# Unread matmuls in TensorE's waits of a recurrent layer, an early output projection, and 512-column matmuls in block 1

## The chip, the cores and the metric

The kernel runs on one core of a Trainium2 chip. The metric is device microseconds for one execution. Engines: TensorE (PE in the profile; its weight loads are PEld), VectorE (DVE), ScalarE (ACT), GpSimd (POOL) and SyncE (SP), which issues the large loads.

## The reference, cut to what matters

256 tokens of width 1024, float32 throughout. Two blocks run one after the other.

```python
# block 1: two layers, each a mix of three branches
proj = rmsnorm(x, norm_g) @ w_in        # 256 x 1024 times 1024 x 8704
aq, ak, av, az, buv, bz, cq, ck, cv, cz, gl = split_cols(proj)
...                                      # two attentions, a gated unit
x = x + merged @ w_out
# block 2: 16 meta tokens + 256 tokens; two layers of ffn, mixer, ffn
h = h + 0.5 * swiglu_ffn(rms_norm(h, ..), ..)
h = h + mixer(rms_norm(h, ..))           # layer 0: attention + delta rule
h = h + 0.5 * swiglu_ffn(rms_norm(h, ..), ..)   # layer 1: rwkv7_time_mix
# rwkv7_time_mix, 16 heads of 64
xr, xw, xk, xv, xa, xg = [h + xx * mu[i] for i in range(6)]
r, k, v = xr @ w_r, xk @ w_k, xv @ w_v   # and three low-rank products
S = S * w_t + sa * b_t + v_t * k_t       # a recurrence over the tokens
y = S @ r_t                              # then a norm per head and a bonus
return (y * g) @ w_o
```

## The kernel before, in words

**Products.** A float32 product is made of three float32r matmuls that add in one PSUM bank: high part by high part, high by low, low by high (`mm3`, L216 to L220: L218, L219, L220). The weights come as units of 512 KB, 128 x 1024, in the order in which the kernel uses them (`Stream`, L192 to L213): SyncE issues the load into `wraw` (four buffers), ScalarE copies it to `wh` (L210, three buffers), VectorE or GpSimd subtracts to get `wl` (L212, three buffers).

**Block 1.** `block1_layer` runs for each of the two layers. In it `proj_tok` (L387 to L406) makes seven of the projections, q, k and v of the two attentions and one more: tokens are the stationary side (`xh`, `xl`, 128 tokens of one k-tile), and a half of the 512 output columns is the moving side. So one projection is two column halves `p`, two halves of k `kh`, two token halves `i`, four k-tiles, three matmuls of 256 columns each, into two banks. Each unit holds four k-tiles of 256 columns. The generator yields after each group of three, and a `Weave` runs other work of the layer between the yields. The order of the units in memory is written by the host (L1824 to L1832).

**Order and banks.** An instruction made through `Pinned` (L88 to L96) stays behind the instruction that was traced before it on its engine; all its records have line L96. All other instructions are put in order by a scheduler. PSUM is eight banks of 128 x 512 float32; `bank(c, tag)` takes the next bank of a ring that the tag names, each bank is a buffer tag of its own with one buffer, and its tiles are handed out in the order in which they were traced.

**The rwkv layer** (`rwkv`, L1479 to L1776, 272 tokens). Its head: statistics of the norm (`rms_scale`, TensorE lines L264), `replicate` of the scale to all partitions (L278 transposes through `rtok`), then the six mixes (L1512 to L1527, VectorE with halves on ScalarE and GpSimd), the three large projections and the low-rank ones. Then eight pairs of heads, j = 0 to 7, in five chunks of 64 tokens, run as a pipeline of three stages written out in a loop:

```python
for s in range(KT + 3):
    if 1 <= s <= KT:
        stage_b(s - 1, Cs[s - 1])
    if s >= 3:
        stage_c(s - 3, Cs[s - 3])
    if s < KT:
        Cs[s] = stage_a(s)
```

`stage_a` (L1650 to L1704) scales the operands on VectorE, makes the products of the pair (L1677: `bbd`, then `kbd`, each five of 128 x 128 in two tiles with tag `sm`), masks them on VectorE, reduces to `iUc` (L1690), transposes (L1696) and makes the bonus (L1702, `mk`). `sm` is a ring of two banks. `stage_b` inverts a triangle per chunk (`tri_inverse`, L910 to L953): 15 rounds of three small VectorE instructions (L923, L924, L925), a mask to `iY` (L927), then two levels of transposes (L937) and products (L946) on TensorE with VectorE's L949 and L951. `stage_c` (L1709 to L1763) runs the recurrence over the chunks (L1715 to L1737), then the norm of the heads (L1743, L1747) and the elementwise end that leaves `kk` and `kp`, the high and the low part of the pair's output (L1762 on ScalarE, L1763 on GpSimd). Buffers of stage A come round after four pairs; `iY` has two buffers.

**The output projection** (`out_proj`, L1779 to L1793) is called behind the loop (L1773) for 256 tokens with the tags `sm` and `iv`. It has eight units of 128 output rows; each adds eight head pairs, k = 0 to 7, three matmuls a pair, and VectorE adds the result to `h` (L1791).

Of the kernel before, what the change touches and what calls it, by code (L numbers as in the profile page):

```python
# [16 lines left out]
P = 128  # L17
D = 1024
KT = 8
# [60 lines left out]
def banks(c, **n):  # L80

    free = sorted(range(8), key=lambda i: c.used[i])
    c.banks = {}
    for tag, k in n.items():
        c.banks[tag], free = free[:k], free[k:]


class Pinned:  # L88
# [167 lines left out]
def rms_scale(c, acc, tok, r=None):  # L256

    nc = c.nc
    tt = tok_tiles(tok)
    nt = len(tt)  # L260
    ps = bank(c, "sm")
    for i, a in enumerate(tt):
        for q, t in enumerate(acc):
            nc.tensor.matmul(ps[:, i:i + 1], t[:, a:a + P], c.cmean, start=q == 0, stop=q == len(acc) - 1)  # L264
    ms = T(c, c.np_, [P, 4], F32, "ms")
    nc.vector.tensor_scalar_add(ms[:, :nt], ps[:, :nt], EPS)
    if r is None:
        r = T(c, c.np_, [P, 4], F32, "rtok")
    nc.gpsimd.tensor_tensor(r[:, :nt], ms[:, :nt], c.mhalf[:, :nt], ALU.pow)
    return r  # L270


def replicate(c, r, tok, R=None):

    nc = c.nc
    ps = bank(c, "sm")
    for i, a in enumerate(tok_tiles(tok)):
        nc.tensor.matmul(ps[:, a:a + P], r[:, i:i + 1].to_broadcast([P, P]), c.ident, start=True, stop=True)  # L278
    if R is None:
        R = T(c, c.np_, [P, tok], F32, "R", bufs=1)  # L280
    nc.scalar.activation(R, ps[:, :tok], AF.Copy)
    return R
# [89 lines left out]
def block1_layer(c, l, xT, head, pos, ws, w_br, w_out, sgu_w, sgu_b, sgu_gb):  # L372

    nc, tc, ap, tp = c.nc, c.tc, c.b1a, c.b1t
    lam_init = 0.8 - 0.6 * math.exp(-0.3 * l)
    xh, xl, acc = head
# [6 lines left out]
    def next_unit():  # L383
        unit[0] += 1
        return ws.unit(unit[0] - 1)

    def proj_tok(evac):  # L387

        pss = [bank(c), bank(c)]
        for p in range(2):  # L390
            for kh in range(2):
                wh, wl = next_unit()
                wh4 = wh.rearrange("p (m k c) -> p m k c", m=2, k=4)
                wl4 = wl.rearrange("p (m k c) -> p m k c", m=2, k=4)
                for i in range(2):
                    o = pss[i][:, 256 * p:256 * p + 256].rearrange("p (m c) -> p m c", m=2)
                    for k4 in range(4):
                        k = 4 * kh + k4
                        a, b = xh[:, k, P * i:P * i + P], xl[:, k, P * i:P * i + P]
                        h, w = wh4[:, :, k4, :], wl4[:, :, k4, :]  # L400
                        pe.matmul(o, a, h, start=k == 0, stop=False)
                        pe.matmul(o, a, w, start=False, stop=False)
                        pe.matmul(o, b, h, start=False, stop=k == 7)
                        if p and kh and k4 == 3:
                            evac(i, pss[i])
                        yield  # L406

    def rope_T(res, scale):

# [1069 lines left out]
def rwkv(c, h, acc, a):  # L1479
# [19 lines left out]

    with ExitStack() as fst:  # L1500
        fp = fst.enter_context(tc.tile_pool(name="rwf", bufs=1, reuse_waits="tile"))
        r = rms_scale(c, acc, TOK2)
        R = replicate(c, r, TOK2)
        lora1, lora2, wrkv = Stream(c, a["rw_lora1"]), Stream(c, a["rw_lora2"]), Stream(c, a["rw_rkv"])
        z1h, z1l = T(c, fp, [P, TOK2], F32R, "z1h"), T(c, fp, [P, TOK2], F32R, "z1l")
        zgh, zgl = T(c, fp, [P, 2, TOK2], F32R, "zgh"), T(c, fp, [P, 2, TOK2], F32R, "zgl")
# [113 lines left out]
    ys = []  # L1620
# [29 lines left out]
    def stage_a(j):  # L1650
        C = Ctx()
        D = Dall[:, j]
        E1 = T(c, pp, [P, NCH, 65], F32, "E1")
        nc.scalar.activation(E1, D, AF.Exp)
        E2 = T(c, pp, [P, NCH, 64], F32, "E2")
        nc.scalar.activation(E2, D[:, :, 1:], AF.Exp, scale=-1.0)
        C.fc = T(c, pp, [P, 4, 1], F32, "fc", bufs=4)
        nc.vector.tensor_sub(C.fc, D[:, 0:4, 64:65], D[:, 1:5, 0:1])
        nc.scalar.activation(C.fc, C.fc, AF.Exp)

        w = j % 4
        AR, Br, Kr, Ka = C.AR, C.Br, C.Kr, C.Ka = arp[w], brp[w], krp[w], kap[w]
        C.abd, C.bt, C.vt, C.kt = abdp[w], btp[w], vtp[w], [t[:, q] for c0, n, t in ktp[w] for q in range(n)]
        nc.vector.scalar_tensor_tensor(AR[:, :, 0, :], chv("kk", j), -1.0, E1[:, :, 0:64], ALU.mult, ALU.mult)
        halves(lambda o, x, p: nc.vector.tensor_mul(o, x, E2[p:p + 64]), bbd, chv("ba", j))
        nc.vector.tensor_mul(AR[:, :, 1, :], chv("r", j), E1[:, :, 1:65])
        halves(lambda o, x, p: nc.gpsimd.tensor_mul(o, x, E2[p:p + 64]), kbd, chv("kp", j))
        halves(lambda o, x, p: nc.scalar.activation(o, x, AF.Copy), C.abd, AR[:, :, 0, :])
        halves(lambda o, x, p: nc.gpsimd.tensor_copy(o, x), vbd, chv("v", j))

        Ub = C.Ub = ubp[j % 3]
        U16 = T(c, pp, [P, NCH, 64], F32, "fk")
        for bd, oa, orr in ((bbd, Ub, Br), (kbd, Ka, Kr)):
            for c0, m in ((0, 4), (4, 1)):
                ps = bank(c, "sm")
                for q in range(m):
                    nc.tensor.matmul(ps[:, P * q:P * q + P], pair_ht(bd[:, c0 + q]), pair_ht(AR[:, c0 + q]),  # L1677
                                     start=True, stop=True)
                p4 = ps[:, :P * m].rearrange("p (c a t) -> p c a t", a=2, t=64)
                if oa is Ub:  # L1680
                    nc.vector.tensor_mul(U16[:, c0:c0 + m, :], p4[:, :, 0, :],
                                         c.m16.unsqueeze(1).to_broadcast([P, m, 64]))
                if oa is Ka or c0 == 0:
                    nc.vector.tensor_mul(oa[:, c0:c0 + m].rearrange("p c (h t) -> p c h t", h=2),
                                         p4[:, :, 0:1, :].to_broadcast([P, m, 2, 64]),
                                         c.mU.rearrange("p (h t) -> p h t", h=2).unsqueeze(1).to_broadcast([P, m, 2, 64]))
                nc.vector.tensor_mul(orr[:, c0:c0 + m, :], p4[:, :, 1, :], c.mR.unsqueeze(1).to_broadcast([P, m, 64]))
            if oa is Ub:
                C.Uc = T(c, pp, [P, NCH, 16], F32, "iUc", bufs=3)
                nc.vector.tensor_reduce(C.Uc, U16.rearrange("p i (b c) -> p i c b", c=16), AX.X, ALU.add)  # L1690

        for bd, parts in ((bbd, [(0, 4, C.bt)]), (kbd, ktp[w]), (vbd, [(0, 4, C.vt), (4, 1, C.vt[:, 4:])])):
            for c0, m, tk in parts:
                ps = bank(c, "sm")
                for q in range(m):
                    nc.tensor.transpose(ps[:, P * q:P * q + P], pair_ht(bd[:, c0 + q]), c.ident)  # L1696
                nc.scalar.activation(tk[:, :m, :], ps[:, :P * m].rearrange("p (c d) -> p c d", d=P), AF.Copy)

        mk = T(c, pp, [P, NCH, 64], F32, "fk").rearrange("p c t -> p (c t)")[:, :TOK2]
        nc.vector.scalar_tensor_tensor(mk, tok("r", j), col(c, "r_k", j), tok("kp", j), ALU.mult, ALU.mult)  # L1700
        ps = bank(c, "sm")
        nc.tensor.matmul(ps[:, :TOK2], c.bo, mk, start=True, stop=True)  # L1702
        nc.vector.tensor_mul(tok("r", j), ps[:, :TOK2], tok("v", j))
        return C  # L1704
# [61 lines left out]
    for s in range(KT + 3):  # L1766
# [3 lines left out]
            stage_c(s - 3, Cs[s - 3])  # L1770
        if s < KT:
            Cs[s] = stage_a(s)
    acc2 = out_proj(c, h, ys, a["rw_out"], ("sm", "iv"), 16)  # L1773
    pst.close()
    st.close()
    return acc2  # L1776


def out_proj(c, h, ys, w_out, tags=("mm",), t0=0):  # L1779

    nc = c.nc
    wo = Stream(c, w_out)
    acc2 = []
    n = TOK2 - t0
    for m in range(KT):
        wh, wl = wo.unit(m)
        ps = bank(c, tags[m % len(tags)])
        for k in range(KT):
            mm3(c, ps[:, :n], wh[:, P * k:P * k + P], wl[:, P * k:P * k + P], *[y[:, t0:] for y in ys[k]],
                k == 0, k == KT - 1)  # L1790
        nc.vector.tensor_add(h[:, m, t0:], ps[:, :n], h[:, m, t0:])  # L1791
        sumsq(c, acc2, h[:, m, t0:], m, n)
    return acc2  # L1793
# [21 lines left out]
def b1_host(I):  # L1815
# [8 lines left out]
    order = []  # L1824
    for nm in ["cq", "ck", "cv", "aq", "ak", "av", "bz", "bu", "bv", "cz", "gC", "gB", "az", "gA"]:
        if nm[1] in "qkv":
            for p in range(2):
                for kh in range(2):
                    order += [(4 * kh + k4, base[nm] + 2 * p + m) for m in range(2) for k4 in range(4)]
        else:  # L1830
            for m in range(8 if nm[0] == "g" else 4):
                order += [(k, base[nm] + m) for k in range(8)]  # L1832
# [131 lines left out]
```

## Time and profile before

| what | us |
|---|---|
| three runs | 2038.01, 2035.98, 2027.44 (median 2035.98) |
| the profiled execution | 2033.22 |
| its span | 2031.5 |
| TensorE busy | 1929.5 (95%) |
| VectorE busy | 1390.8 (68%) |
| ScalarE busy | 973.2 (48%) |
| GpSimd busy | 285.1 (14%) |

Mean granted clock of TensorE in the profiled execution: 0.964 of its full speed. Times in the rows below are microseconds from the span's start. Matmuls are pipelined, so a matmul's own duration is longer than the distance from it to the next; a rate is read from starts. A row of the timeline is the start, the duration of the group, engine, line, operation, what is written from what, the tile and the count; in brackets how long the engine was idle before it and what ended that.

### The profile page before, as it was taken

What the parts mean: (1) busy time and instruction counts of PE and PEld (TensorE: products, weight loads), DVE (VectorE), ACT (ScalarE), POOL (GpSimd) and SP (SyncE); (2) the same over time, 40 slices, a digit from 0 to 9 for tenths busy, and PEclk for the clock granted to TensorE, in tenths of its full rate; (3) what the DMA queues carried; (4) which work ended last, traced back from release to release, by engine and by line L of the source; (5) the groups of instructions that cost most, each with busy time, mean ns of one, the idle gap of its engine ahead of it and who ended that gap; (6) DMA issues with size and microseconds to landing.
All of it is one profiled execution on the core that took longest, in us unless ns stands there. A gap on an engine that the chain in (4) does not pass through costs nothing.

```text
span 2031.5 us, 37801 instructions
## 1 busy us (share of the span) xinstructions
PE 1929.5 (95%) x15003; PEld 1858.0 (91%) x15003; DVE 1390.8 (68%) x2896; ACT 973.2 (48%) x1745; POOL 285.1 (14%) x320
## 2 busy tenths in 40 slices
PE   8999999999999999968999999999989879989998
PEld 7889999889999999966999999999988768979998
DVE  6577576577578665787477665666589699846764
ACT  5455355455355444442354444444366535555443
POOL 1113011113010000143010000000044313110000
PEclk9999899999899999987999999999989789989999
DMA  6445466445455555532235555555534100026663
GB/s 200 137 123 160 142 180 181 142 117 161 141 177 176 177 175 174 164 107 63 63 112 169 175 175 176 171 175 174 171 94 135 42 12 1 32 72 180 186 186 115
DMA packets 79461, 280.02 MB, mean 138 GB/s; under 512 B 9890, under 2 KB 12082, under 8 KB 79156
## 3 DMA queue, kind: packets, MB, share of 16 engines
q1 hardware_dynamic: 77088, 275.57, 45.5%
q8 instruction: 118, 1.93, 0.4%
q10 hardware_dynamic: 2196, 2.03, 0.3%
q14 instruction: 59, 0.48, 0.1%
HBM read 276.50 MB, written 1.07 MB: 137 GB/s over the span
## 4 chain that ended last, share of the span: by engine, by line
PE 64%; DVE 9%; ACT 2%; POOL 2%; issue 1%; DVEq 0%; ACTq 0%; POOLq 0%
PE mm L220 17%; PE mm L218 16%; PE mm L219 16%; PE mm L96 4%; PE iv L96 1%; PE iv L946 1%; DVE wl L212 1%; PE fs L96 1%; PE sm L1677 1%; DVE mixt L1523 1%; DVE iYc L925 1%; DVE ish L924 1%; DVE ish L923 0%; PE sm L264 0%; ACT wh L210 0%
## 5 line engine op out<-in xcount | busy, mean ns | idle before, releaser
L210 ACT ACTIVATE wh<-wraw 128x1024 fp32r<-128x1024 f32 x517 | 546.9, 1059 | 603.6 <-PE mm L219 288.8
L212 DVE TENSOR_TENSOR wl<-wraw,wh 128x1024 fp32r<-128x1024 f32 x474 | 587.1, 1239 | 254.9 <-ACT wh L210 249.6
L218 PE MATMUL mm<-xh,wh 128*128 128x272 f32 (+1 forms) x2112 | 607.4, 288 | 5.9 <-ACT xh L1524 3.0
L220 PE MATMUL mm<-xh,wl 128*128 128x272 f32 (+1 forms) x2112 | 606.2, 287 | 6.6 <-DVE wl L212 2.9
L219 PE MATMUL mm<-xl,wh 128*128 128x272 f32 (+1 forms) x2112 | 606.9, 287 | 0.9 <-POOL xl L1526 0.9
L220 PEld LDWEIGHTS mm<-xh,wl 128*128 128x128 f32 x2112 | 401.5, 190 | 9.0 <-DVE wl L212 5.1
L218 PEld LDWEIGHTS mm<-xh,wh 128*128 128x128 f32 x2112 | 399.7, 189 | 7.9 <-ACT xh L1524 3.5
L219 PEld LDWEIGHTS mm<-xl,wh 128*128 128x128 f32 x2112 | 401.1, 190 | 1.9 <-POOL xl L1526 1.3
L218 PE MATMUL mm<-uh,wh 128*128 128x272 f32 (+1 forms) x704 | 201.7, 286 | 0.0
L219 PE MATMUL mm<-ul,wh 128*128 128x272 f32 (+1 forms) x704 | 201.5, 286 | 0.0
L220 PE MATMUL mm<-uh,wl 128*128 128x272 f32 (+1 forms) x704 | 201.0, 286 | 0.0
L212 POOL TENSOR_TENSOR wl<-wraw,wh 128x1024 fp32r<-128x1024 f32 x43 | 103.0, 2396 | 412.4 <-ACT wh L210 368.8
L96 PE MATMUL mm<-wh,xh 128*128 128x256 f32 x448 | 133.9, 299 | 9.2 <-ACT wh L210 9.2
L220 PEld LDWEIGHTS mm<-uh,wl 128*128 128x128 f32 x704 | 133.2, 189 | 0.0
L218 PEld LDWEIGHTS mm<-uh,wh 128*128 128x128 f32 x704 | 132.3, 188 | 0.0
L219 PEld LDWEIGHTS mm<-ul,wh 128*128 128x128 f32 x704 | 132.3, 188 | 0.0
L96 PE MATMUL mm<-wl,xh 128*128 128x256 f32 x448 | 127.4, 284 | 0.7 <-DVE wl L212 0.7
L96 PE MATMUL mm<-wh,xl 128*128 128x256 f32 x448 | 126.6, 283 | 0.0
L96 PE MATMUL mm<-xh,wh 128*128 128x272 f32 (+1 forms) x360 | 120.0, 333 | 0.0
L96 PE MATMUL mm<-xh,wl 128*128 128x272 f32 (+1 forms) x360 | 107.0, 297 | 0.0
L96 PE MATMUL mm<-xl,wh 128*128 128x272 f32 (+1 forms) x360 | 106.8, 297 | 0.0
L96 PEld LDWEIGHTS mm<-wh,xh 128*128 128x128 f32 x448 | 86.1, 192 | 9.2 <-ACT wh L210 9.2
(597 smaller groups left out, 3576.9 us busy)
## 6 DMA issues: line engine op xcount, KB each, us to landing
wraw<-in_ffn_in SPq DMA_DIRECT2D x176, 512.0 KB, 3.6
wraw<-in_w_in SPq DMA_DIRECT2D x136, 512.0 KB, 3.7
wraw<-in_ffn_out SPq DMA_DIRECT2D x88, 512.0 KB, 3.7
wraw<-in_hyb_in SPq DMA_DIRECT2D x29, 512.0 KB, 3.7
wraw<-in_w_br SPq DMA_DIRECT2D x24, 512.0 KB, 3.8
wraw<-in_rw_rkv SPq DMA_DIRECT2D x24, 512.0 KB, 3.8
wraw<-in_w_out SPq DMA_DIRECT2D x16, 512.0 KB, 4.4
wraw<-in_hyb_out SPq DMA_DIRECT2D x8, 512.0 KB, 3.7
```

The lines of the kernel that those rows point to most:

```text
L96: return lambda *a, **k: self.tc.keep_in_program_order(f(*a, **k))
L210: nc.scalar.activation(wh, r, AF.Copy)
L212: eng.tensor_sub(wl, r, wh.bitcast(F32))
L218: pe.matmul(ps, lh, rh, start=start, stop=False)
L219: pe.matmul(ps, lh, rl, start=False, stop=False)
L220: pe.matmul(ps, ll, rh, start=False, stop=stop)
L924: nc.vector.tensor_mul(sh, sh, Uc[:, :, j:j + 1].to_broadcast([n, ni, 16 - j]))
L925: nc.vector.tensor_add(Yc[:, :, j:], Yc[:, :, j:], sh)
L946: pe.matmul(ps[:n, n * i:n * i + n], lhs[:, i0 + i, :], rhs[:, i0 + i, :], start=True, stop=True)
L1523: nc.vector.scalar_tensor_tensor(t, xx[:, k, :], col(c, "mu", 8 * i + k), hn[:, k, 1:], ALU.mult, ALU.add)
L1677: nc.tensor.matmul(ps[:, P * q:P * q + P], pair_ht(bd[:, c0 + q]), pair_ht(AR[:, c0 + q]), start=True, stop=True)
```

## The change

It has three parts. First, `fill` makes n bf16 matmuls of 128 x 512 from a constant into one bank; nothing reads the bank. In the rwkv layer five stand behind `rms_scale` and twelve behind `replicate` (tag `mm`); in `stage_a` of pairs 0 to 2 they stand ahead of the products (14 for pair 0, 4 for pairs 1 and 2) and five ahead of the transposes (tag `sm`). All are pinned. Second, `out_proj` adds head pairs 0 to 6 of its first three units, pinned, and then for each of them pair 7; the other five units are as before, pinned too. Third, `proj_tok` takes two k-tiles of all 512 columns a unit, so a matmul has 512 columns; it yields after the second and the third matmul of a group, 32 times a projection as before; the host writes the units in that order.

```diff
+def fill(c, n, tag="sm", pe=None):
+
+    ps = bank(c, tag)
+    for _ in range(n):
+        (pe or c.nc.tensor).matmul(ps, c.identb, c.identb.unsqueeze(1).to_broadcast([P, 4, P]), start=True, stop=True)
...
     def proj_tok(evac):
 
         pss = [bank(c), bank(c)]
-        for p in range(2):
-            for kh in range(2):
-                wh, wl = next_unit()
...
-                        pe.matmul(o, a, h, start=k == 0, stop=False)
-                        pe.matmul(o, a, w, start=False, stop=False)
-                        pe.matmul(o, b, h, start=False, stop=k == 7)
...
+        for kq in range(4):
+            wh, wl = next_unit()
+            for i in range(2):
+                for k2 in range(2):
+                    k = 2 * kq + k2
+                    a, b = xh[:, k, P * i:P * i + P], xl[:, k, P * i:P * i + P]
+                    h, w = wh[:, 512 * k2:512 * k2 + 512], wl[:, 512 * k2:512 * k2 + 512]
+                    pe.matmul(pss[i], a, h, start=k == 0, stop=False)
+                    pe.matmul(pss[i], a, w, start=False, stop=False)
+                    yield
+                    pe.matmul(pss[i], b, h, start=False, stop=k == 7)
+                    if k == 7:
+                        evac(i, pss[i])
+                    yield
...
+        pe = Pinned(c, nc.tensor)
         r = rms_scale(c, acc, TOK2)
+        fill(c, 5, "mm", pe)
         R = replicate(c, r, TOK2)
+        fill(c, 12, "mm", pe)
...
+        if j < 3:
+            fill(c, 14 if j == 0 else 4, "sm", pe)
         Ub = C.Ub = ubp[j % 3]
...
+        if j < 3:
+            fill(c, 5, "sm", pe)
         for bd, parts in ((bbd, [(0, 4, C.bt)]), (kbd, ktp[w]), (vbd, [(0, 4, C.vt), (4, 1, C.vt[:, 4:])])):
...
-    acc2 = out_proj(c, h, ys, a["rw_out"], ("sm", "iv"), 16)
+    acc2 = out_proj(c, h, ys, a["rw_out"], ("sm", "iv"), 16, 3)
...
-def out_proj(c, h, ys, w_out, tags=("mm",), t0=0):
+def out_proj(c, h, ys, w_out, tags=("mm",), t0=0, early=0):
...
+    pe = Pinned(c, nc.tensor) if early else nc.tensor
...
+    part = {}
+
+    def add(m, ks):
+        if m not in part:
+            part[m] = wo.unit(m), bank(c, tags[m % len(tags)])
+        (wh, wl), ps = part[m]
+        for k in ks:
+            mm3(c, ps[:, :n], wh[:, P * k:P * k + P], wl[:, P * k:P * k + P], *[y[:, t0:] for y in ys[k]],
+                k == 0, k == KT - 1, pe)
+        return ps
+
+    for m in range(early):
+        add(m, range(KT - 1))
     for m in range(KT):
...
+        ps = add(m, [KT - 1] if m < early else range(KT))
```

## Rows read from the trace of the kernel before

**Rows 1.** The page: busy time of the engines, PEclk by 40 slices, and the chain.

```profile
PE 1929.5 (95%) x15003; PEld 1858.0 (91%) x15003; DVE 1390.8 (68%) x2896; ACT 973.2 (48%) x1745; POOL 285.1 (14%) x320
...
PEclk9999899999899999987999999999989789989999
...
PE 64%; DVE 9%; ACT 2%; POOL 2%; issue 1%; DVEq 0%; ACTq 0%; POOLq 0%
```

**Rows 2.** Windows: window, length, busy (instructions) of each engine, PEclk, DMA share, GB/s.

```profile
60.00:160.00 100.00, 99.50 (x765) 89.98 (x764) 68.22 (x160) 49.33 (x109) 15.56 (x8) 1.00 0.42 126
...
700.00:800.00 100.00, 100.00 (x800) 100.00 (x799) 63.45 (x90) 48.11 (x65) 0.00 (x0) 1.00 0.59 175
1840.00:1940.00 100.00, 100.00 (x843) 100.00 (x842) 71.58 (x109) 50.80 (x73) 0.00 (x0) 1.00 0.62 184
```

**Rows 3.** Timeline of TensorE in block 1's projections, at full clock.

```profile
34.97 0.28 PE L96 MATMUL mm<-wl,xh 128*128 128x256 f32 x1
...
35.91 0.28 PE L96 MATMUL mm<-wh,xh 128*128 128x256 f32 x1
```

**Rows 4.** Groups of instructions: count, busy time, mean ns, idle time before.

```profile
L96 PE MATMUL mm<-wh,xh 128*128 128x256 f32 x448 | 133.9, 299 | 9.2 <-ACT wh L210 9.2
```

**Rows 5.** Timeline of TensorE at the head of the rwkv layer.

```profile
1468.99 1.65 PE L278 MATMUL sm<-ident,rtok 128*128 128x128 f32 x6 [1.18 <-POOL rtok L269]
1473.65 1.05 PE L218 MATMUL mm<-xh,wh 128*128 128x272 f32 x3 [3.02 <-ACT xh L1524]
```

**Rows 6.** Timeline of TensorE, stage A of the first pairs.

```profile
1605.45 2.47 PE L1677 MATMUL sm<-wh,bbd 128*128 128x128 f32 x10 [4.01 <-DVE wh L1666]
...
1617.00 1.27 PE L1677 MATMUL sm<-wh,bbd 128*128 128x128 f32 x5
...
1640.14 1.92 PE L1677 MATMUL sm<-xh,bbd 128*128 128x128 f32 x10
```

**Rows 7.** Windows of the head pairs; columns as in rows 2.

```profile
1605.00:1640.00 35.00, 27.31 (x113) 23.28 (x114) 28.91 (x124) 13.63 (x29) 9.42 (x13) 0.55 0.00 1
...
1670.00:1700.00 30.00, 28.91 (x232) 26.90 (x231) 27.08 (x118) 18.30 (x53) 6.81 (x8) 1.00 0.01 1
```

**Rows 8.** Timeline of VectorE in the inversions: rounds, L927 and L951.

```profile
1642.28 0.82 DVE L927 TENSOR_TENSOR iY<-iYc,bm 128x640 f32<-128x640 f32 x1
...
1654.63 0.69 DVE L951 TENSOR_TENSOR iY<-iv,iY 128x512 f32<-128x512 f32 x1 [0.17 <-PE iv L946]
...
1670.78 0.19 DVE L923 STREAM_SHUFFLE ish<-iYc 128x35 f32<-128x35 f32 x1
...
1671.48 0.19 DVE L923 STREAM_SHUFFLE ish<-iYc 128x40 f32<-128x40 f32 x1
...
1674.50 0.83 DVE L927 TENSOR_TENSOR iY<-iYc,bm 128x640 f32<-128x640 f32 x1
...
1752.44 0.18 DVE L923 STREAM_SHUFFLE ish<-iYc 128x20 f32<-128x20 f32 x1
...
1753.24 0.19 DVE L923 STREAM_SHUFFLE ish<-iYc 128x25 f32<-128x25 f32 x1
```

**Rows 9.** Timeline of TensorE where the recurrence of pair 0 ends.

```profile
1674.06 0.41 PE L1720 MATMUL ch<-r,iY 128*128 128x128 f32 x2
```

**Rows 10.** The output projection: groups of 1775 to 1804 us, then timelines of TensorE, ScalarE.

```profile
L218 PE MATMUL sm<-kk,wh 128*128 128x256 f32 x9 | 2.9, 324 | 1.0 <-ACT kk L1762 1.0
...
1804.42 0.72 PE L1747 MATMUL ch<-ysb,bo 128*128 128x272 f32 x2 [0.95 <-ACT ysb L1746]
1811.36 0.58 PE L218 MATMUL sm<-kk,wh 128*128 128x256 f32 x1 [6.22 <-ACT kk L1762]
...
1818.75 0.38 PE L219 MATMUL iv<-kp,wh 128*128 128x256 f32 x1
1818.96 0.29 PE L220 MATMUL iv<-kk,wl 128*128 128x256 f32 x1
...
1812.81 1.06 ACT L210 ACTIVATE wh<-wraw 128x1024 fp32r<-128x1024 f32 x1 [1.50 <-PE sm L219]
```

More of the change, by code (lines that the diff above doesn't have):

```diff
@@ L389, in proj_tok @@
         pss = [bank(c), bank(c)]
-        for p in range(2):
-            for kh in range(2):
-                wh, wl = next_unit()
[L393 to L400, printed above, removed]
-                        pe.matmul(o, a, h, start=k == 0, stop=False)
-                        pe.matmul(o, a, w, start=False, stop=False)
-                        pe.matmul(o, b, h, start=False, stop=k == 7)
-                        if p and kh and k4 == 3:
-                            evac(i, pss[i])
-                        yield
+        for kq in range(4):
[12 more added lines that the diff above has]
+                    yield
     def rope_T(res, scale):
@@ L1784, in out_proj @@
     n = TOK2 - t0
-    for m in range(KT):
[L1786 to L1790, printed above, removed]
+    part = {}
[9 more added lines that the diff above has]
+        add(m, range(KT - 1))
+    for m in range(KT):
+        ps = add(m, [KT - 1] if m < early else range(KT))
         nc.vector.tensor_add(h[:, m, t0:], ps[:, :n], h[:, m, t0:])
@@ L1826, in b1_host @@
         if nm[1] in "qkv":
-            for p in range(2):
-                for kh in range(2):
-                    order += [(4 * kh + k4, base[nm] + 2 * p + m) for m in range(2) for k4 in range(4)]
+            order += [(k, base[nm] + m) for k in range(8) for m in range(4)]
         else:
```

## The prediction

> **What bounds the kernel now.** The page comes first. TensorE is busy 95% of the span, VectorE 68%, and the chain that ended last runs through TensorE for 64% and VectorE for 9% [rows 1]. So time is won either by giving TensorE less to do, or by shortening the stretches in which it isn't the engine that ends last. The PEclk line shows where those are: nine in most slices, six to eight in a few, which is TensorE at its lower clock for part of the slice [rows 1]. Next, the windows of block 1 and of the large products of block 2: PE is busy 99.50 us of 100 in block 1 and all of it in block 2's products, at a granted clock of 1.00 [rows 2]. There only the matmuls' own spacing counts. The windows of the rwkv layer's head pairs look different: from 1605 to 1640 us VectorE is busy 28.91 us of 35, TensorE 27.31 of 35 at a mean clock of 0.55; from 1670 to 1700 VectorE is busy 27.08 of 30 with TensorE at full clock [rows 7]. In this layer VectorE's chains set the pace. A matmul that nobody reads can only help there where TensorE's own time ends a wait, and it hurts where real work stands behind it.
>
> **512 columns in block 1.** Each of the 14 projections goes from 96 matmuls of 256 columns to 48 of 512: three groups of 448 like the one in [rows 4], 1344 in all, become 672, with the same columns, weight bytes and units. At full clock neighbours stand 0.12 us apart; finer, from 34.97 to 35.91 us there are eight steps, 0.1175 us each [rows 3]. 256 columns at 2.4 GHz take 0.1067 us, so a matmul costs 10.8 ns beside its columns. At the lower clock the step is 0.21 us (1818.75 to 1818.96 in [rows 10]), which is 256 columns at 1.2 GHz and nothing beside them. A second pair of rows agrees: 800 matmuls of 272 columns in 100 us make 125.0 ns, 843 of 256 columns make 118.6 [rows 2]; 16 columns are worth 6.4 ns, which is 6.67 at 2.4 GHz, so the rest, 11.7 to 11.9 ns, doesn't grow with columns between these two widths. The trace has no float32r matmul of 512 columns. Bounds: nothing, if the 11 ns do grow; 672 x 11.9 = 8.0 us if all that is saved is the fixed part. TensorE is busy through, so the saving counts in full, except in the first projection, part of which runs at the lower clock. I take 672 x 11.2 ns, between the two readings, = **-7.5 us**. The Trainium skill (TensorE: Matmul & The Clock Gate, section "Wait — 56ns, not 53.3ns?") gives a warm matmul a fixed 2.5 ns above its columns; by that the part would be worth 672 x 2.5 ns = 1.7 us and the sum would end near 2037. The steps of this trace show four times as much [rows 3], so the sum goes by the trace. The new order of the units changes which four units a projection takes, not how many; the DMA runs as before and costs nothing while TensorE is busy.
>
> **Head of the rwkv layer.** After the statistics TensorE waits 1.18 us for `rtok` and, after `replicate`, 3.02 us for `xh` [rows 5]. The 5 and 12 unread matmuls of 512 bf16 columns stand there. The trace has no bf16 matmul of this width; with 512 columns at 2.4 GHz and the fixed part above I estimate 0.2245 us each, 17 make 3.8 us against 4.2 us of waiting: they fit. At the lower clock they take 0.427 us, the first five 2.1 us, and `replicate` comes up to 1 us late. What they may give back: TensorE runs at the lower clock for the first products behind 1473.65. But those products then wait for VectorE's mixes, so little is won. I take **+0.2 us** (-0.5 to +1).
>
> **Stage A of pairs 0 to 2.** The first product, at 1605.45, comes after a wait of 4.01 us for `wh`, VectorE's [rows 6]. Fourteen unread matmuls last 14 x 0.225 = 3.1 us, so they fit at full clock; at the lower one (6.0 us) they delay pair 0 by about 2 us. If the clock stays up, pair 0's own matmuls, which take 11.6 us from 1605.45 to 1617.00 with 10 products in 2.47 us, get shorter by about 2.8 us. That is the gain: VectorE's first chain starts earlier.
>
> The loss lies in the order. The fills are pinned: each stays behind the TensorE instruction traced before it. For pairs 1 and 2 that is the last product of `stage_b` of the pair before, L946. And the fill takes an `sm` bank. A bank's tiles are handed out in traced order, and there are two: so from the second product tile of pair 1 on, stage A of pair 1 waits until pair 0's inversion has ended; likewise pair 2 behind pair 1. In the kernel before, products of pair 3 start at 1640.14 [rows 6], two microseconds before the first inversion's VectorE rounds end at 1642.28 [rows 8]: all three stage As ran ahead, and VectorE interleaved their rounds. What is that worth? Two chains interleaved take 0.80 us for a round of each (1752.44 to 1753.24), one alone 0.70 us (1670.78 to 1671.48) [rows 8]. A chain run alone thus leaves about 0.30 us a round unused, 15 rounds a chain, two chains: 9 us. Behind the rounds an inversion has two levels on TensorE, 12.4 us from L927 at 1642.28 to L951 at 1654.63 [rows 8], in which VectorE, without rounds of a next pair, is idle for about 5 us by my estimate (masks, evictions and the next pair's scaling take the rest); twice makes 10. The upper price is 19 us. Against it stand the 2.8 us of the clock and, above all, that pair 0's inversion, no longer sharing VectorE, ends some 20 us sooner: 15 x 0.70 = 10.5 us of rounds from about 1610, where its first products are done [rows 6], and then 12.4 make 1633 instead of 1655, and `stage_c` of pair 0 starts there. `stage_c` is what frees the two `iY` buffers: pair 2's mask at 1674.50 stands right behind pair 0's last L1720 at 1674.06 [rows 8, 9]. Its work fills VectorE where the missing rounds leave holes, and VectorE's work is the same in sum. From 1670 to 1700 VectorE is idle for a tenth of the time [rows 7]; over the 40 us behind that could give back 4 us at most, so the lower bound is -2.8 - 4 = -7. Of the 19 us I let `stage_c` fill ten, about half, since it starts 20 us sooner but has chains of its own through TensorE: 19 - 2.8 - 10 = **+6 us** (-7 to +19), the wide term of the sum.
>
> **The output projection.** In words the change adds seven head pairs of three units ahead of the last pair. The trace shows that this order already runs: between 1775 and 1804 us there are nine products of `kk` with `wh` in `sm` alone [rows 10], ahead of the wait for the last pair. What changes is where they stand: they are pinned behind the last product of `stage_c` of pair 7, at 1804.42, where TensorE then waits 6.22 us for `kk` [rows 10]. 63 x 0.1175 = 7.4 us fill that wait to the end and 1.2 us over; what stands behind them is the last pair's part of the three units, and then unit 3, whose copy to `wh` started at 1812.81 [rows 10], when unit 0 had let go of its buffer, and does so again, so TensorE is not held longer by that overrun than by the weights. The wait also cost the clock: from 1811.36 to 1818.96 matmuls stand 0.21 us apart [rows 10], some 30 of them, each 0.095 us too long: 2.9 us, which a busy wait saves. Net: 2.9 saved, 1.2 spent, -1.7, and at best 0.8 more from pairs 6 and 7 with no other matmuls between theirs. Against it, the 63 no longer fill TensorE's gaps before 1804, so that stretch may fall to the lower clock and the first fills with it (+2). I take **-1 us** (-2.5 to +2).
>
> **Sum.** -7.5 + 0.2 + 6 - 1 = -2.3 us. The profiled execution took 2033.2 us, 2.8 below the median of the runs and inside their spread (2027.4 to 2038.0); so I forecast **2031 us**.
>
> **Rivals.** 0.5% is about 10 us; less than that can hardly be told from no change here.
> *The order costs nothing* (0.27). VectorE is the bound of the layer, its work is the same, and `stage_c` fills every hole; the clock then stays up through the head too. -7.5 - 2.8 - 2 - 0.5 is about -13: **2020 us**. For it: VectorE at 90% in [rows 7]. Against: 0.70 us for a round alone [rows 8].
> *The order costs its full price* (0.18). Pairs 1 and 2 start behind pairs 0 and 1 and nothing fills the holes: 19 + 0.2 - 7.5 - 1 = +10.7: **2044 us**, slower, and 2047 with the output projection at its bound of +2. It decides from the point where stage A's term passes +18. For it: the two-bank ring and the traced order; against it: `stage_c`'s earlier start.
> *512 columns give nothing* (0.10). The fixed part grows with the columns, as if the engine moved 256 columns in 0.1175 us whatever the split: 0 + 0.2 + 6 - 1 = +5.2: **2038 us**. Against it: the step from 256 to 272 columns [rows 2]. The Trainium skill's figure in the section named above lies next to this rival; no run here shows it yet.
> *The output projection does not do what it says* is part of every case: its head pairs already run ahead [rows 10], so its worth is only the clock behind 1811.
> The forecast, between the first two, has 0.45.
>
> **Range.** From all lower bounds, -8 - 0.5 - 7 - 2.5 = -18, and a microsecond for the spread of runs, 2014, to 2047 of the slow rival. Faster 0.28 (the fast rival and the forecast's edge), slower 0.20 (the slow rival and the other edge), the same 0.52. The likeliest case alone: 2024 to 2038.
>
> **What would show it.** In block 1: spacing of 512-column matmuls near 0.2245 us and block 1's end some 7.5 us sooner. In the head: fills ending before `xh`, and 1473.65's successor not later. In stage A: whether products of pair 1 stand behind L946 of pair 0, when pair 2's L927 comes against 1674.50, and when the last L1747 comes against 1804.42 (less the shift of block 1). At the end: no clock drop behind the last L1747. I am wrong if 512 columns take 0.235 us; if pair 1's products run ahead of the fill; or if the last L1747 moves by more than 10 us beside block 1's shift.

## The result, and the profile after

The changed kernel takes 2054.86 us (median of four runs, 2051.81 to 2056.25) against 2034.78 us of the kernel before: a ratio of 1.0099, 95% interval 1.0079 to 1.0118, some 20 us slower. The forecast was 2031 us, its range ended at 2047; the time lies above the range, on the other side of no change. Lines in the rows below are those of the changed kernel: `Pinned` is L103 now (L96 before), the mask to `iY` L931 (L927), the inversion's products L950 (L946), stage A's products L1686 (L1677), `iUc` L1699 (L1690), the last product of stage C L1758 (L1747).

Where the 20 us came from is read from starts that both traces have (those of the weight loads, which lead their matmuls by up to 0.2 us). The rwkv layer's statistics start at 1465.1 before and at 1460.1 after: 5 us gained up to there. The next layer's statistics start at 1831.0 and 1853.7: 27.7 us lost inside the rwkv layer. Of that, 2.9 us lie between its statistics and stage A's first product (1605.4 and 1603.3), 26.3 us between that product and the last product of stage C (1804.5 and 1828.7), and -1.4 us in the output projection (26.5 and 25.1 us).

The page of the changed kernel hardly differs: busy time of the engines, the clock by slices, and the chain.

```profile
PE 1944.0 (95%) x14385; PEld 1823.7 (89%) x14385; DVE 1394.3 (68%) x2896; ACT 976.0 (48%) x1745; POOL 290.7 (14%) x320
...
PEclk9999999999999999988999999999989789999999
...
PE 83%; DVE 10%; ACT 2%; POOL 2%; issue 2%; DMA 0%; DVEq 0%; ACTq 0%; POOLq 0%
```

TensorE is 14.5 us busier, VectorE as busy as before; nothing here tells where the time is [rows 1]. The windows of the head pairs do (columns as in rows 2):

```profile
1605.00:1640.00 35.00, 17.87 (x90) 14.50 (x91) 22.02 (x89) 6.56 (x15) 3.14 (x4) 0.71 0.00 0
1640.00:1670.00 30.00, 23.73 (x134) 18.69 (x132) 20.64 (x87) 11.64 (x30) 2.80 (x4) 0.84 0.06 18
1670.00:1700.00 30.00, 24.44 (x144) 20.05 (x145) 20.09 (x91) 8.72 (x23) 8.79 (x12) 0.82 0.00 1
```

VectorE, busy 28.91 us from 1605 to 1640 and 27.08 from 1670 to 1700 before [rows 7], is busy 22.02 and 20.09 now: it waits. What it waits for is in TensorE's timeline, from pair 0's stage A to pair 1's:

```profile
1603.50 1.28 PE L1686 MATMUL sm<-wh,bbd 128*128 128x128 f32 x10
...
1618.14 1.13 PE L1686 MATMUL sm<-wh,kbd 128*128 128x128 f32 x8 [1.75 <-DVE iYc L929]
1625.96 1.12 PE L941 MATMUL iv<-ident,iY 128*128 128x128 f32 x4 [6.70 <-DVE iY L931]
...
1638.20 2.08 PE L950 MATMUL iv<-iY,iP 128*128 128x128 f32 x8 [0.78 <-DVE iP L953]
1640.08 1.91 PE L103 MATMUL sm<-identb 128*128 128x512 bf16 x4
1641.78 0.64 PE L1731 MATMUL ch<-r,iY 128*128 128x128 f32 x2
1642.21 0.63 PE L1686 MATMUL sm<-wh,bbd 128*128 128x128 f32 x2
```

Pair 1's first tiles (eight products each at 1615.23 and 1618.14) ran early. The four pinned fills at 1640.08 stand right behind the last L950 of pair 0's inversion, and the last two `bbd` products of pair 1, whose tile is the next turn of the fills' bank, behind the fills at 1642.21. So do the last two `kbd` products, at 1643.72, while the eight at 1618.14, in the ring's other bank, ran early. Without those two there is no `iUc`, and without it no rounds for pair 1:

```profile
1643.15 0.69 DVE L1699 TENSOR_REDUCE iUc<-fk 128x80 f32<-128x320 f32 x1
...
1662.86 0.82 DVE L931 TENSOR_TENSOR iY<-iYc,bm 128x640 f32<-128x640 f32 x1
...
1704.25 0.82 DVE L931 TENSOR_TENSOR iY<-iYc,bm 128x640 f32<-128x640 f32 x1
```

Pair 0's mask comes at 1625.08, 17 us earlier than before; pair 1's comes 37.8 us behind it, pair 2's, at 1704.25, 41.4 us behind that, against 1674.50 before [rows 8]. Three inversions stand in a row. Cut into rounds and levels, from one mask or `iUc` to the next (columns as in rows 2):

```profile
1606.10:1625.10 19.00, 7.61 (x50) 5.88 (x50) 17.63 (x79) 5.08 (x12) 3.14 (x4) 0.85 0.00 1
1625.10:1643.10 18.00, 13.35 (x49) 10.46 (x50) 4.20 (x10) 1.47 (x3) 0.00 (x0) 0.50 0.00 0
1643.10:1662.90 19.80, 15.08 (x106) 12.66 (x105) 17.12 (x80) 7.43 (x20) 2.80 (x4) 1.00 0.09 28
1662.90:1682.10 19.20, 15.17 (x56) 11.65 (x57) 5.45 (x14) 6.26 (x15) 3.05 (x4) 0.56 0.00 0
```

In the rounds VectorE is nearly full (17.63 of 19.00, 17.12 of 19.80): the holes that a lone chain leaves are filled by masks and scaling. In the levels it is busy 4.20 us of 18.00 and 5.45 of 19.20, and TensorE's clock is granted at half (0.50, 0.56): 13.8 + 13.8 = 27.6 us in which VectorE has nothing to do. In pair 0's levels its masks and sums wait for TensorE's products, the first two like this:

```profile
1629.88 0.69 DVE L953 TENSOR_TENSOR iP<-iv,moff 128x512 f32<-128x512 f32 x1 [3.49 <-PE iv L950]
1632.74 0.69 DVE L955 TENSOR_TENSOR iY<-iv,iY 128x512 f32<-128x512 f32 x1 [2.17 <-PE iv L950]
```

That these levels are where the loss lies shows in the whole stretch of the head pairs. The windows are those of the kernel before, of the changed kernel and of the kernel without the fills of pairs 1 and 2, which is the first experiment below:

```profile
1605.42:1804.52 199.10, 177.20 (x1270) 160.76 (x1270) 156.08 (x699) 93.25 (x255) 43.35 (x58) 0.91 0.05 17
...
1603.28:1828.67 225.39, 181.94 (x1232) 157.14 (x1231) 161.44 (x699) 94.10 (x253) 43.20 (x57) 0.90 0.05 15
...
1606.84:1799.03 192.19, 163.45 (x1214) 146.16 (x1213) 158.85 (x699) 93.09 (x254) 43.25 (x57) 0.97 0.06 18
```

VectorE is idle for 43.0, 63.9 and 33.3 us in them. Against the kernel before, the loss of 26.3 us is 20.9 us more of idle time and 5.4 us by which the same number of VectorE instructions, 699, took longer; against the third kernel the loss is 33.2 us, 30.6 of them idle time.

### The profile page after: what moved, and what is told of

It reads as the page before. It is cut to its first block, busy times and chain, and to the rows that moved or that the text cites. A ratio compares the mean times of both kernels' runs of the same rounds, so it can differ in the third digit from the quotient of the medians.

```text
span 2054.5 us, 36572 instructions
## 1 busy us (share of the span) xinstructions
PE 1944.0 (95%) x14385; PEld 1823.7 (89%) x14385; DVE 1394.3 (68%) x2896; ACT 976.0 (48%) x1745; POOL 290.7 (14%) x320
## 4 chain that ended last, share of the span: by engine, by line
PE 83%; DVE 10%; ACT 2%; POOL 2%; issue 2%; DMA 0%; DVEq 0%; ACTq 0%; POOLq 0%
PE mm L227 19%; PE mm L226 19%; PE mm L225 19%; PE mm L103 13%; PE sm L103 3%; PE iv L103 2%; PE iv L950 1%; DVE wl L219 1%; PE po L103 1%; PE fs L103 1%; DVE ish L928 1%; DVE mixt L1530 1%; DVE iYc L929 1%; DVE ish L927 1%; PE sm L1686 1%
## 5 line engine op out<-in xcount | busy, mean ns | idle before, releaser
L219 POOL TENSOR_TENSOR wl<-wraw,wh 128x1024 fp32r<-128x1024 f32 x43 | 107.5, 2501 | 404.2 <-ACT wh L217 370.9
L103 PE MATMUL mm<-xh,wh 128*128 128x272 f32 (+1 forms) x360 | 119.9, 333 | 0.0
L103 PE MATMUL mm<-xh,wl 128*128 128x272 f32 (+1 forms) x360 | 106.9, 297 | 0.0
L103 PE MATMUL mm<-xl,wh 128*128 128x272 f32 (+1 forms) x360 | 106.9, 297 | 0.0
L103 PE MATMUL mm<-wh,xh 128*128 128x512 f32 x224 | 95.0, 424 | 9.0 <-ACT wh L217 9.0
L226 PE MATMUL mm<-yl,wh 128*128 128x256 f32 x320 | 91.2, 286 | 0.5 <-DVE yl L235 0.5
L227 PE MATMUL mm<-yh,wl 128*128 128x256 f32 x320 | 90.8, 284 | 0.0
L103 PE MATMUL mm<-wh,xl 128*128 128x512 f32 x224 | 90.5, 404 | 0.0
```

The lines of the kernel that those rows point to most:

```text
L103: return lambda *a, **k: self.tc.keep_in_program_order(f(*a, **k))
L219: eng.tensor_sub(wl, r, wh.bitcast(F32))
L226: pe.matmul(ps, lh, rl, start=False, stop=False)
L227: pe.matmul(ps, ll, rh, start=False, stop=stop)
```

## The experiments

The comparisons are ratios to the kernel before on the same chip. Runs of the kernel before lay between 2019 and 2042 us, so where a few microseconds matter stretches of the traces stand beside the times.

**Is it the fills of pairs 1 and 2, and is it their place or their time?** First they are left out:

```diff
-        if j < 3:
-            fill(c, 14 if j == 0 else 4, "sm", pe)
+        if j < 1:
+            fill(c, 14, "sm", pe)
...
-        if j < 3:
+        if j < 1:
             fill(c, 5, "sm", pe)
```

> The changed kernel without the unread matmuls of pairs 1 and 2 (both groups); those of pair 0, the head, the early output projection and the 512 columns stay. Theory A (order: a pinned fill in an sm bank holds stage A of pairs 1 and 2 behind the inversion of the pair before): the 26 us between the first product of stage A and the last L1758 go, so about 2055 - 26 = 2029 us, and pair 1's products stand ahead of pair 0's L950. Theory B (the fills' own time on TensorE): 18 fills at 0.22 to 0.43 us are 4 to 8 us, so 2047 to 2051 us.

Measured: 2023.82 us, ratio 0.9958 (0.9930 to 0.9987), by the two ratios 29 us less than the changed kernel. The head pairs take 192.2 us from the first product to stage C's last one, against 225.4 with the fills and 199.1 before. 18 matmuls can't cost that by their own time. Then the same number of fills, pinned as before, but in a bank of the inversion's own ring:

```diff
-            fill(c, 14 if j == 0 else 4, "sm", pe)
+            fill(c, 14 if j == 0 else 4, "sm" if j == 0 else "iv", pe)
```

> The changed kernel, but the four fills ahead of the products of pairs 1 and 2 go to an iv bank in place of an sm bank; as many fills, pinned as before. Theory A (order through the sm banks): stage A of pairs 1 and 2 is free again, about 2029 to 2033 us. Theory B (the fills' own time, or the pin alone): unchanged, 2055 us.

Measured: 2026.89 us, ratio 0.9964 (0.9938 to 0.9990), head pairs 194.0 us. The fills' time and the pin stay, the loss is gone. In its trace the four fills of pair 1 again stand behind pair 0's inversion, but all ten of pair 1's first products ran 29 us ahead of them:

```profile
1615.99 2.30 PE L1686 MATMUL sm<-wh,bbd 128*128 128x128 f32 x10
...
1644.40 1.16 PE L950 MATMUL iv<-iY,iP 128*128 128x128 f32 x8
1645.39 1.03 PE L103 MATMUL iv<-identb 128*128 128x512 bf16 x4
```

And the other way round, in the kernel before, one narrow matmul with no time to speak of:

```diff
+    for _ in range(n):
+        (pe or c.nc.tensor).matmul(ps[:, :16], c.identb, c.identb[:, :16], start=True, stop=True)
...
+        if 1 <= j < 3:
+            fill(c, 1, "sm", Pinned(c, nc.tensor))
         Ub = C.Ub = ubp[j % 3]
```

> The kernel before, with nothing of the change but one unread matmul of 16 columns, pinned, in an sm bank, ahead of the products of pairs 1 and 2. It has hardly any time of its own. Theory A (order): 2035 + 26 to 30 = 2061 to 2065 us. Theory B (own time): 2035 us.

Measured: 2060.31 us, ratio 1.0134 (1.0087 to 1.0180): +27 us (18 to 37), from two matmuls of 16 columns; the head pairs take 222.6 us. TensorE's timeline in this kernel, where the first of them stands:

```profile
1652.64 2.08 PE L953 MATMUL iv<-iY,iP 128*128 128x128 f32 x8 [0.78 <-DVE iP L956]
1654.51 0.22 PE L103 MATMUL sm<-identb 128*128 128x16 bf16 x1
1654.81 0.80 PE L1686 MATMUL sm<-wh,bbd 128*128 128x128 f32 x2
```

Again the inversion's last products, the pinned matmul, and only then the two products of pair 1. With one pair alone:

```diff
-        if 1 <= j < 3:
+        if j == 1:
```

> The kernel before with one pinned matmul of 16 columns ahead of the products of pair 1 alone. If each inversion that is set in a row costs its own latency: about half of the 23 to 27 us that the order costs with pairs 1 and 2, so +10 to +14 and 2045 to 2048 us. If VectorE's lost time is the price, as the prediction had it: 4.5 + 5 less what stage C fills, +3 to +9, 2037 to 2043 us.

Measured: 2049.36 us, ratio 1.0069 (1.0037 to 1.0102): +14 us (8 to 21), half of the price of two, as the reading by latency had it. The other reading's upper edge, +9, is inside the interval; the trace decides: the head pairs take 214.1 us, 15 more than before, and 194.4 to 199.1 in the five kernels that have no unread matmul there. Pair 0's mask and pair 1's, 47.6 us behind it:

```profile
1626.39 0.82 DVE L934 TENSOR_TENSOR iY<-iYc,bm 128x640 f32<-128x640 f32 x1
...
1673.96 0.82 DVE L934 TENSOR_TENSOR iY<-iYc,bm 128x640 f32<-128x640 f32 x1
```

Pair 2's follows 14.2 us later, since its rounds were free to run beside pair 1's.

**Does it take the pin, the bank, or both?** The four fills without the pin:

```diff
-            fill(c, 14 if j == 0 else 4, "sm", pe)
+            fill(c, 14 if j == 0 else 4, "sm", pe if j == 0 else None)
```

> The changed kernel with the four fills ahead of the products of pairs 1 and 2 still in an sm bank but not pinned. If it takes the pin and the bank together to hold stage A: 2024 to 2029 us, with the fills early. If a tile more in the ring is enough: 2050 us or more.

Measured: 2020.36 us, ratio 0.9939 (0.9921 to 0.9958), the lowest median of this study. Its timeline of TensorE, where the unpinned fills have line L92:

```profile
1609.16 0.72 PE L1713 MATMUL sm<-fk,bo 128*128 128x272 f32 x2 [2.04 <-ACT vt L1708]
1609.72 1.03 PE L92 MATMUL sm<-identb 128*128 128x512 bf16 x4
1610.81 1.38 PE L1686 MATMUL sm<-wh,bbd 128*128 128x128 f32 x10
...
1626.10 0.61 PE L941 MATMUL iv<-ident,iY 128*128 128x128 f32 x4
```

The bank is the same, the tile in the ring too; without the pin the fills run at 1609.72, between pair 0's last stage A matmul and pair 1's first, 16 us ahead of pair 0's first level at 1626.10. So it takes both: a pin behind late work, and a buffer that early work needs next. And the five fills ahead of the transposes, which are pinned behind products of their own pair, with the four left out:

```diff
-        if j < 3:
-            fill(c, 14 if j == 0 else 4, "sm", pe)
+        if j < 1:
+            fill(c, 14, "sm", pe)
         Ub = C.Ub = ubp[j % 3]
...
         if j < 3:
             fill(c, 5, "sm", pe)
```

> The changed kernel without the four fills ahead of the products of pairs 1 and 2, but with the five ahead of their transposes, which stand behind products of the same pair. If only the place behind the other pair's inversion costs: 2024 to 2029 us. If any pinned fill in an sm bank there costs: 2035 us or more.

Measured: 2022.64 us, ratio 0.9948 (0.9923 to 0.9973), head pairs 189.9 us. These pinned fills in the same banks cost nothing.

**What are 512 columns worth?** Forty unread float32r matmuls of each width, one after the other, at the start of the fourth projection of the kernel before:

```diff
+                if c.proj == 4 and p == kh == 0:
+                    for m in (64, 128, 256, 384, 512):
+                        for _ in range(40):
+                            pe.matmul(pss[0][:, :m], xh[:, 0, :P], wh[:, :m], start=True, stop=True)
```

> The kernel before, with 200 unread float32r matmuls more at the start of the fourth projection of block 1: 40 each of 64, 128, 256, 384 and 512 columns, into the bank that the projection then overwrites. By the prediction's reading (columns at 2.4 GHz and 11 ns a matmul) the steps are 0.038, 0.064, 0.118, 0.171 and 0.224 us. By the other reading (0.448 ns a column and some 3 ns a matmul, from the steps 0.1175 and 0.232 of the two kernels) they are 0.031 or the weight load's own time, 0.060, 0.118, 0.175 and 0.232 us. The kernel as a whole gets 200 matmuls longer: about 2035 + 25 = 2060 us.

Measured once: 2065.05 us. Windows inside the stretches of 64, 128, 256, 384 and 512 columns (columns as in rows 2; the counts include the matmuls that hang over an edge):

```profile
50.50:54.50 4.00, 4.00 (x38) 4.00 (x37) 0.54 (x2) 2.82 (x4) 0.00 (x0) 1.00 0.77 291
57.00:63.00 6.00, 6.00 (x30) 6.00 (x29) 0.00 (x0) 0.00 (x0) 0.65 (x1) 0.50 0.30 88
64.00:68.00 4.00, 4.00 (x21) 4.00 (x21) 0.00 (x0) 0.00 (x0) 0.00 (x0) 0.50 0.00 0
71.00:77.00 6.00, 6.00 (x37) 6.00 (x36) 0.00 (x0) 0.00 (x0) 0.00 (x0) 1.00 0.01 3
78.00:86.00 8.00, 8.00 (x36) 6.45 (x35) 0.00 (x0) 0.00 (x0) 0.00 (x0) 1.00 0.00 0
```

From the starts of the forty: 64 columns 0.112 us a step at full clock, 128 columns 0.2135 at half, 256 the same 0.2135 at half, 384 0.1735 and 512 0.2333 at full. At the lower clock 128 columns take as long as 256, and at full clock 64 take nearly as long, so below 256 columns these matmuls get hardly cheaper; from 256 on their time goes with the columns: 0.1175 / 256 = 0.459, 0.1735 / 384 = 0.452, 0.2333 / 512 = 0.456 ns a column.

The floor goes with the stationary side, as rows of the kernel before show, all at full clock. Float32 matmuls of a single column on 128 stationary columns stand 0.11 us apart (0.22 for two), and six of 64 columns on 96 stationary columns 0.08 us (0.65 us less the last one's own 0.25, over five steps):

```profile
20.47 0.36 PE L264 MATMUL sm<-cmean,sq 128*128 128x1 f32 x2
20.69 0.36 PE L264 MATMUL sm<-cmean,acc 128*128 128x1 f32 x2
...
970.38 0.65 PE L96 MATMUL po<-fvt,fpT 96*96 96x64 f32 x6
```

So there is hardly a fixed part to save: two of 256 columns take 0.235 us [rows 3], and in the changed kernel one of 512 takes 18 steps from 29.73 to 33.91, 0.232 us:

```profile
29.73 0.40 PE L103 MATMUL mm<-wl,xh 128*128 128x512 f32 x1
...
33.91 0.40 PE L103 MATMUL mm<-wl,xh 128*128 128x512 f32 x1
```

The part alone:

```diff
-            for p in range(2):
-                for kh in range(2):
-                    order += [(4 * kh + k4, base[nm] + 2 * p + m) for m in range(2) for k4 in range(4)]
+            order += [(k, base[nm] + m) for k in range(8) for m in range(4)]
```

(with the changed `proj_tok`, as in the diff above)

> The kernel before with the 512-column matmuls of block 1 and the new order of units alone. By the prediction's reading -7.5 us, 2026 to 2028 us, and the two layers of block 1 end 7.5 us sooner in the trace. By the ladder's reading (512 columns take 0.233 us, two of 256 take 0.235) 672 x 0.002 to 0.003 = 1.3 to 2 us, so no change that can be told, and block 1 ends 1 to 2 us sooner beside what its stretches at the lower clock change.

Measured: 2033.27 us, ratio 0.9980 (0.9963 to 0.9997). That is 4 us, less than the 7.5 and more than the 2 expected. The traces are compared where the clock was at half for the same time, 10.2 us in each layer of block 1. From its statistics to the next ones the first layer then takes 308.3 to 308.8 us in four kernels with 256 columns and 306.6 to 307.7 in four with 512, 1.38 us less as a mean; the second takes 300.4 to 300.7 us in six and 299.3 to 299.5 in four, 1.16 us less. Together that is 2.5 us, 3.8 ns for each of the 672 matmuls saved. The 4 us of the runs agree with it within their interval, 0.6 to 7.5 us.

**The output projection alone**, the rest as before:

```diff
-    acc2 = out_proj(c, h, ys, a["rw_out"], ("sm", "iv"), 16)
+    acc2 = out_proj(c, h, ys, a["rw_out"], ("sm", "iv"), 16, 3)
```

> The kernel before with the pinned early output projection alone. The prediction's term is -1 us; from the traces of both kernels, 26.5 against 25.1 us from the last product of the head pairs to the statistics behind the projection, so -1.4 us, and nothing in the pairs themselves; with the seven pairs' products no longer in the gaps of pairs 6 and 7, at worst +2.

Measured: 2034.91 us, ratio 0.9988 (0.9971 to 1.0005). From stage C's last product to the next statistics it takes 26.6 us, as before the change. The windows just before and after that product show the clock:

```profile
1800.00:1805.30 5.30, 3.20 (x19) 2.16 (x17) 0.35 (x1) 2.21 (x6) 0.82 (x2) 1.00 0.00 0
1805.30:1808.70 3.40, 3.40 (x14) 3.17 (x15) 0.89 (x2) 1.60 (x4) 0.00 (x0) 0.50 0.00 0
1808.70:1815.00 6.30, 6.30 (x55) 6.30 (x54) 0.00 (x0) 1.32 (x3) 3.09 (x4) 1.00 0.00 0
```

With the projection's matmuls moved out of pair 7's gaps TensorE is busy 3.20 us of 5.30, the clock falls just as the 63 matmuls begin, and the first of them run at half. In the changed kernel it didn't fall there and the stretch took 25.1 us. Over all the traces, seven with the early order and seven without, the stretch took 25.1 to 27.7 us with it and 25.1 to 26.6 without, 26.1 and 26.2 as means: 25.1 in three of the seven with it, where the clock stayed up, and 26.6 to 27.7 in the four where it fell. So in this stretch the order is worth nothing as a mean.

**The head alone**, the rest as before:

```diff
+        fill(c, 5, "mm", pe)
         R = replicate(c, r, TOK2)
+        fill(c, 12, "mm", pe)
```

> The kernel before with the 5 and 12 unread matmuls of the head alone. The prediction's term is +0.2 us (-0.5 to +1). In the changed kernel the first mixed product came 0.5 us later after the statistics than before; I expect the same here, and the stretch up to stage A within 2 us of the 140.3 us of before: the first products run at full clock but then wait for VectorE. If the clock is worth something there: 3 to 5 us less.

Measured: 2035.28 us, ratio 1.0001 (0.9986 to 1.0017); from the statistics to stage A 140.8 us against 140.3, and 140.2 to 143.4 in the other kernels, with fills in the head and without. TensorE's clock there is higher with them (0.83 as a mean from 1466 to 1476 us, 0.52 before from 1467 to 1477), and no gain in time comes of it.

**Pair 0's fills alone**, the rest as before:

```diff
+        if j < 1:
+            fill(c, 14, "sm", pe)
         Ub = C.Ub = ubp[j % 3]
...
+        if j < 1:
+            fill(c, 5, "sm", pe)
```

> The kernel before with the 14 and 5 unread matmuls of pair 0 alone. In the kernel without the fills of pairs 1 and 2 the head pairs took 192.2 us against 199.1. If that comes from pair 0's fills: about -7 us in that stretch (the prediction had -2.8 and at best -7). If it comes from the early output projection's order or from chance: 199 us again.

Measured: 2028.13 us, ratio 0.9963 (0.9941 to 0.9984); head pairs 193.7 us against 199.1. Of the parts tried alone this one gains most, 7.5 us by the runs (3 to 12). Its trace, the slowest of its five executions, doesn't show where: the head pairs took 194.4 to 199.1 us in the five kernels without unread matmuls there, 194.4 in the one with the early output projection alone; stage A's first product comes 143.4 us behind the statistics, 3.1 later than before; and from the rwkv layer's statistics to the next ones it took 363.3 us, against 363.8 to 366.4 in those five. What is clear in it is the clock: at half for 10.2 us of the head pairs, and for 16.9 to 36.1 us in the five.

**The parts that don't cost, together:** the kernel without the fills of pairs 1 and 2, and without the head's.

```diff
-        fill(c, 5, "mm", pe)
         R = replicate(c, r, TOK2)
-        fill(c, 12, "mm", pe)
```

> The version with the parts that paid alone: 512 columns, pair 0's fills, the early output projection; no fills in the head and none for pairs 1 and 2. The sum of the parts by their own runs is 0.998 x 0.9988 x 0.9963 = 0.993, so about 2020 us; with the head's fills it was 0.9958.

Measured: 2023.58 us, ratio 0.9959 (0.9936 to 0.9982), within its interval the same as with the head's fills. The sum of the parts, 0.993, was not reached in the time. The kernels with the unpinned fills (0.9939) and with the second fills alone (0.9948) are ahead by less than the intervals tell apart; all of them beat both kernels.

## Why the prediction was wrong, step by step

**Stage A of pairs 0 to 2** is the step that failed, by its size and not by its mechanism. That a pinned fill in an `sm` bank holds stage A of the next pair behind the inversion is what the trace shows (1640.08 to 1642.21) and what the experiments confirm: no loss in another bank, none without the pin, 27 us from two matmuls of 16 columns. It held the second and the fourth product tile, which share the fills' bank, and not all "from the second product tile of pair 1 on". The prediction named this as the slow rival at 18 in 100. Its term had three wrong numbers. "VectorE, without rounds of a next pair, is idle for about 5 us by my estimate" in the levels of an inversion: it was 13.8 us, since the levels with what stands around them took 18 to 19 us at the lower clock and not 12.4, and nothing else was ready. "About 0.30 us a round unused", 9 us in all: VectorE was idle 1.4 and 2.7 us in two stretches of rounds, which took 19.0 and 19.8 us and not 10.5, since masks and scaling of the other pairs ran between them; with the longer levels, pair 0's inversion ended 14 us sooner than before and not some 20. And "of the 19 us I let `stage_c` fill ten": stage C of pair 0 can't fill pair 0's own levels, because it starts behind them, and through pair 1's levels (1662.90 to 1682.10) it left VectorE 5.45 us busy of 19.20. Against the +6 us of the term, with 19 as its upper bound, the order alone cost 27 us (18 to 37), and order and time of the fills together 29.

The gain in the same term was sized too low. Pair 0's fills were given 2.8 us for the shorter matmuls; alone they are worth 0.37% (0.16 to 0.59), 7.5 us. That this is near the lower bound of -7 is luck: 4 of those 7 us were meant for `stage_c` in VectorE's holes. The clock did stay up as forecast; where the rest of the 7.5 us is won the traces don't show.

**512 columns** were put at -7.5 us; the traces make it 2.5, the runs 4 (0.6 to 7.5). The step that failed is "256 columns at 2.4 GHz take 0.1067 us, so a matmul costs 10.8 ns beside its columns". The division took the row's rate for a rate of 2.4 GHz; float32r at full clock took 0.455 ns a column in every row from 256 columns up, and nearly all of the difference was no fixed part. The rows at hand had two widths only 16 columns apart: 6.4 ns for 16 columns was read as 6.67, and 16 x 0.455 = 7.3 was not thought of, though a step of 0.1175 us and one of 0.1186 for the same 256 columns [rows 2, 3] show that the difference isn't known to a nanosecond. The section "Wait — 56ns, not 53.3ns?" of the Trainium skill's TensorE: Matmul & The Clock Gate, which the prediction set aside, gives some 2.5 ns a matmul beside its columns. For the bf16 fills the trace agrees: they stand 0.216 us apart at full clock, and 512 / 2.4 + 2.5 = 215.8 ns is the estimate by that figure. For float32r of 512 columns it doesn't give the 0.232 us, but its small fixed part is nearer to what was saved (3.8 ns a matmul) than the prediction's 11.2.

**The head** was right: the fills fit into the waits, 0 us (0.2 forecast). The estimate of 0.2245 us a fill was 0.216, and 0.427 at the lower clock as worked out.

**The output projection**: -1 us forecast, -2 (-6 to +1) measured alone, nothing in its own stretch there, -1.4 us in the changed kernel and nothing as a mean of all the traces. That its head pairs ran ahead already was right. That busy matmuls keep the clock up was right in one trace and wrong in another, as the bound of +2 had allowed.

Summed by the runs of the parts alone: -4 (columns), 0 (head), -7.5 (pair 0), +27 (order), -2 (projection), which makes +13.5 against the measured 20; the interval of the order's run alone, 18 to 37, covers the difference. The fills of pairs 1 and 2 have a time of their own besides their order (8 of them at 0.427 us, 10 at 0.216, 5.6 us, on the chain of three inversions in a row); that this is the rest was not tried by itself.

## What to carry to other kernels

An instruction that nobody reads still takes a buffer and a place in an order. Ask of it: behind what is it pinned, when is that done, and who needs the buffer's next turn; a matmul of 16 columns cost 14 us a time. Price a broken overlap by the whole latency that now stands alone, at the clock it will run at, and count as cover only work that is ready then: work that starts behind the same event covers nothing. And don't take a fixed cost from a rate that was assumed: divide two widths far apart.

## What the runs showed of the hardware

With 128 stationary columns a float32r matmul of 64 columns took 0.112 us at full clock and one of 128 columns 0.2135 us at half, about the time of 256 columns either way (0.1175, 0.2135). The floor goes with the stationary side: a single column took 0.11 us on 128 stationary columns, 64 columns took 0.08 us on 96. Behind the forty of 64 columns, through which TensorE was busy 4.00 us of 4.00, the granted clock fell from 1.00 to 0.50 at 54.9 us; it stayed there through the forty of 128 and came back at 68.6, while matmuls of 256 columns ran. And the same code took different times: from block 1's end to the rwkv layer's statistics, which no part of the change touches, the traces of this study took between 831.8 and 844.3 us, longest where the clock was at half for 20.5 and 23.9 us near 920 and 950; it was at half for 34.1 us of the shortest and 61.4 us of the longest. This alone is 12 us, as much as many a term of the sum, and single traces are compared here by stretches for that reason.
